# A tokens' norm summed in four column groups, and the order of the first weight loads

## The chip, the cores and the metric

The kernel runs on one core of a Trainium2 chip. The metric is device time in microseconds of one execution, and lower is better. A core has five engines that run side by side: PE (the matrix engine TensorE, whose weight loads the profile lists apart as PEld), DVE (VectorE), ACT (ScalarE), POOL (GpSimd) and SP (SyncE, which here only issues transfers). Transfers between device memory and on-chip memory run on 16 DMA engines that all queues share. Matmuls write to PSUM, from where DVE and ACT read.

## What is computed

One layer of a block for a generator over latent tokens: 512 tokens of width 2048, and 256 context tokens. Only the head of it matters here:

```python
shift, scale, gate = jnp.split(silu_c @ w_ada[l] + b_ada[l], 3, axis=-1)
shift_c, scale_c, gate_c = jnp.split(silu_cc @ w_ada[l] + b_ada[l], 3, axis=-1)
h = _modulate(_rmsnorm(xs, norm_g[l]), shift[:, None], scale[:, None])
hc = _modulate(_rmsnorm(cs, norm_g[l]), shift_c, scale_c)
...
p = h @ w_l
```

`_rmsnorm` divides each token by the root of the mean of its squares over the 2048 columns, and `_modulate` is `h * (1 + scale) + shift`. Everything behind it (attention with normalised and rotated heads, a Fourier mixer, gates, two projections, a residual add and a last norm) reads `p`, and is not touched by the change.

## The kernel before

Tokens are held transposed: `xt` has the 2048 columns in 16 blocks (`kb`) of 128 partitions, with the 512 tokens along the free axis. All matmuls of the projections run as three passes (`mm3`, lines 251 to 253): each operand is split in a high and a low part (`split_from`, lines 131 and 132: ACT copies the high part, DVE subtracts), and high x high, high x low and low x high are added in PSUM.

The first stage, up to about 215 us, makes `h` block by block and at once multiplies it with the first 14 tiles of the input projection. For each `kb` it needs the following.

- The tokens' norm, once for all blocks. `squares` (line 385) squares the 16 blocks of `xt`, 13 on ACT (line 394) and three on DVE (392), adds them in pairs on DVE (395) and sums over the partitions with eight matmuls against a matrix of ones (397), which leaves each token's sum on all 128 partitions. ACT takes the square root (404) and DVE the reciprocal (405), over 128 x 512 numbers.
- The shift and the gain of the block's 128 columns. `modulation(kb)` multiplies a modulation matrix of 2 MB, loaded in two halves (`wada_load`, line 365, four buffers), with the two conditioning vectors: `matvec` (line 425) uses 32 columns of the array for each of four matmuls. ACT copies the result (432), two transposes turn it to columns (435), DVE sums and scales (439, 487, 488).
- `make_h` (line 412): DVE multiplies the tokens by gain and norm (`ht`, 414), ACT adds the shift for the high part (415), DVE makes the low part (416).

`start_work` then runs the projection's tiles for the groups of blocks of which `h` is complete (1, 1, 2, 4, 4 and 4 blocks), with weights that come as `start` pieces through `start_load` (line 162, on SP's queue, four raw buffers) and are split by lines 131 and 132. Its results are kept by lines 453 and 455.

`warm` (line 445) issues matmuls whose product is never read. In block 0 there are three behind the matrix products and five behind the transposes.

The order of instructions on each engine is set when the program is built, by a scheduler; each engine then works through its own list in order and waits where an operand isn't there. PE's list before is: eight norm matmuls, the first matrix in two halves, three unread products, two transposes, five unread products, the first half of the second matrix, then the first projection tiles. SP's list is: the small vectors, `xt` in six pieces, the first matrix, three start pieces, the second matrix, and then a further start piece whenever a raw buffer is free. The matrices from the third on come through POOL's queue, two blocks ahead, each when PE has freed a buffer.

Of the kernel before, what the change touches and what calls it, by code (L numbers as in the profile page):

```python
# [10 lines left out]
F32 = mybir.dt.float32  # L11
F32R = mybir.dt.float32r
ACT = mybir.ActivationFunctionType
ALU = mybir.AluOpType
# [4 lines left out]
P = 128  # L19
D = 2048  # L20
T = 512
C = 256
KK = D // P
# [38 lines left out]
    f = {"P1": "Z5", "P2": "S2", "Q6": "S3", "P7": "S4"}.get(name)  # L62
    return [(f, pc - 1)] if f and g == 0 and pc in (1, 2) else []

XCH = [(0, 2), (2, 2), (4, 4), (8, 4), (12, 2), (14, 2)]


def start_pieces():
# [15 lines left out]
def block_kernel(ctx, tc, xT, ctxT, x, c_row, w_ss, w_gate, vecs, qkg, rope, dft_c, dft_s,  # L84
                 w_start, w_kv, w_m, w_g, w_pab, w_o, final_g, out):
    nc = tc.nc
    sb = lambda name, bufs=1, side="left": ctx.enter_context(tc.tile_pool(name=name, bufs=bufs, side=side))

    def region(name, side="left", **kw):
        st = ExitStack()  # L90
        return st, st.enter_context(tc.tile_pool(name=name, bufs=1, side=side, **kw))
# [18 lines left out]
    def uid(s):  # L110
        cnt[0] += 1
        return f"{s}{cnt[0]}"
# [3 lines left out]
    def slot(pool, shape, dt=F32):  # L116

        n = turns[pool] = turns.get(pool, -1) + 1
        return pool.tile([P] + list(shape), dt, tag=f"s{n % KK}", bufs=1, name=uid("s"))

    def hm_tile(shape, dt, name):
        return slot(hm, shape[1:], dt)

    def bank(shape=(P, 512)):
        return ps.tile(list(shape), F32, tag="b1", bufs=4, name=uid("pb"))

    def bank2():
        return ps.tile([P, 1024], F32, tag="b2", bufs=2, name=uid("pd"))
# [6 lines left out]
    todo, ahead = [], []  # L135
# [16 lines left out]
    def start_load():  # L152

        e = todo[0]
        used = [p for a in ahead for p, _ in a.raws]
        free = [p for p in raw_pools for _ in range(p[1] - used.count(p))]
        if len(e.parts) > len(free) or e.stage == 0 and (not chain or left[e.pc]):
            return False
        todo.pop(0)
        for p, src in zip(free, e.parts):  # L160
            raw = p[0].tile([P, 1024], F32, tag=p[2], bufs=p[3], name=uid("wr"))[:, : e.cols]
            nc.sync.dma_start(raw, src)
            e.raws.append((p, raw))
        if e.stage == 0:
            nc.sync.dma_start(chain[e.pc], e.first)
            left[e.pc] = 1
        ahead.append(e)
        return True
# [89 lines left out]
    ones = const.tile([P, P], F32, name="ones")  # L258
# [3 lines left out]
    eps_t = const.tile([P, 1], F32, name="eps_t")  # L262
# [4 lines left out]
    cvt, bada, ng = small[:, : 2 * KK], small[:, 2 * KK : 5 * KK], small[:, 5 * KK :]  # L267
# [8 lines left out]
    hhi = [None] * KK  # L276
    hlo = [None] * KK
# [51 lines left out]
    for g in range(4):  # L329
        for name in ONE_GROUP:  # L330
            stream_product(name, g, w_g[g], BY_DVE_GATES)
            if g >= 2 and name in DONE:
                half, c = DONE[name]
# [8 lines left out]
    for name in OUT_GROUP:  # L342
        stream_product(name, 4, w_o[1], BY_DVE_OUT)
        if name in DONE:
            half, c = DONE[name]
            stream(("x", half, 2 + c), flat(x[half, 2 + c]), 1024, 1, "raw")
    for name in ONE_GROUP:
        stream_product(name, 5, w_o[0], BY_DVE_OUT)
        half, c = {"P2": (0, 0), "P7": (1, 1), "Q3": (1, 0)}.get(name, (0, 0))
# [12 lines left out]
    pa, pap = region("pa", "right")  # L362
    xt = pap.tile([P, KK, T], F32, name="xt")

    def wada_load(kb, h):
        w = pap.tile([P, 8, 256], F32, tag="wada", bufs=4, name=uid("wa"))
        (nc.gpsimd if kb > 1 else nc.sync).dma_start(w, w_ss[kb, :, 8 * h : 8 * h + 8, :])
        return w

    for a, n in XCH:  # L370
        nc.sync.dma_start(xt[:, a : a + n, :], xT[:, a : a + n, :])


    c2 = pap.tile([P, KK, 32], F32, name="c2")
    nc.vector.memset(c2, 0.0)
    rt = pap.tile([P, 1], F32, name="rt")
    ce = pap.tile([P, 2 * KK], F32, name="ce")
    nc.scalar.activation(ce, cvt, ACT.Exp, scale=-1.0)
    nc.scalar.activation(rt, ce[:, 0:1], ACT.Sqrt)
    nc.vector.tensor_scalar(ce, ce, 1.0, None, op0=ALU.add)  # L380
    nc.vector.reciprocal(ce, ce)
    nc.vector.tensor_tensor(c2[:, :, 0:2].rearrange("p k j -> p j k"),
                            cvt.rearrange("p (j k) -> p j k", j=2),
                            ce.rearrange("p (j k) -> p j k", j=2), op=ALU.mult)
    def squares(srcs, n, r, new, run=None):

        acc = bank2()
        for q in range(0, KK, 2):
            a, b = new(), new()
            for t, src in zip((a, b), srcs(q)):  # L390
                if run is None and t is b and q in (4, 8, 10):
                    nc.vector.tensor_tensor(t, src, src, op=ALU.mult)
                else:
                    nc.scalar.activation(t, src, ACT.Square)
            nc.vector.tensor_tensor(a, a, b, op=ALU.add)
            if run is None:
                nc.tensor.matmul(acc[:, :n], ones, a, start=q == 0, stop=q == KK - 2)
            elif q == 0:
                nc.vector.tensor_copy(run, a)
            else:  # L400
                nc.vector.tensor_tensor(run, run, a, op=ALU.add)
        if run is not None:
            nc.tensor.matmul(acc[:, :n], ones, run, start=True, stop=True)
        nc.scalar.activation(r, acc[:, :n], ACT.Sqrt, bias=eps_t[:, 0:1], scale=1.0 / D)
        nc.vector.reciprocal(r, r)

    wada = {(0, h): wada_load(0, h) for h in range(2)}
    while todo and len(ahead) < 3:
        start_load()
    wada.update({(1, h): wada_load(1, h) for h in range(2)})  # L410

    def make_h(hi, lo, src, rr, kb, j, pool, n):
        tmp = pool.tile([P, n], F32, tag="htmp", bufs=2, name=uid("ht"))
        nc.vector.scalar_tensor_tensor(tmp, src, gain[:, kb, j : j + 1], rr, op0=ALU.mult, op1=ALU.mult)
        nc.scalar.activation(hi, tmp, ACT.Identity, bias=shift[:, kb, j : j + 1])  # L415
        nc.vector.scalar_tensor_tensor(lo, tmp, shift[:, kb, j : j + 1], hi.bitcast(F32),  # L416
                                       op0=ALU.add, op1=ALU.subtract)

    def matvec(acc, pieces):

        kk = 0
        for w in pieces:
            for k in range(w.shape[1]):
                j = kk % 4
                nc.tensor.matmul(acc[32 * j : 32 * j + 32, :256], c2[:, kk, :], w[:, k, :],
                                 start=kk < 4, stop=kk >= KK - 4)
                kk += 1

    def columns(acc, kb):

        o = pap.tile([P, 256], F32, tag="ada_o", bufs=2, name=uid("ado"))
        nc.scalar.copy(o, acc[:, :256])
        sp = acc[:, 512:768]
        for i in range(2):
            nc.tensor.transpose(sp[:, P * i : P * i + P], o[:, P * i : P * i + P], ident)
        if kb == 0:
            warm(5, o)
        r = pap.tile([P, 2, 2], F32, tag="ada_r", bufs=2, name=uid("adr"))
        nc.vector.tensor_reduce(r, sp.rearrange("p (h g r) -> p h r g", h=2, g=4)[:, :, 0:2, :], axis=AX.X, op=ALU.add)
        return r  # L440

    def warm(n, src):

        for _ in range(n):
            nc.tensor.matmul(wacc[:, :256], ones, src, start=True, stop=True)

    def start_work():
        ends = {kb + nk for kb, nk in GROUPS}
# [32 lines left out]
    def modulation(kb):  # L481
        acc = bank2()
        matvec(acc, pieces := [wada.pop((kb, h), None) or wada_load(kb, h) for h in range(2)])
        if kb == 0:
            warm(3, pieces[1][:, 7, :])
        sp = columns(acc, kb)
        nc.vector.tensor_scalar(shift[:, kb, :], sp[:, 0, :], bada[:, kb : kb + 1], None, op0=ALU.add)
        nc.vector.tensor_scalar(gain[:, kb, :], sp[:, 1, :], bsc1[:, kb : kb + 1], ng[:, kb : kb + 1],
                                op0=ALU.add, op1=ALU.mult)

    wacc = bank()
    rx = pap.tile([P, T], F32, name="rx")
    squares(lambda q: (xt[:, q, :], xt[:, q + 1, :]), T, rx, lambda: hm_tile([P, 2, T], F32, name=uid("sq"))[:, 0, :])
    modulation(0)

    work = start_work()
    done = 0
    for kb in range(KK):
        if kb:
            modulation(kb)  # L500
        if kb % 2 == 0:
            pairs.append([hm_tile([P, 2, T], F32R, name=uid(n)) for n in ("hh", "hl")])
        hhi[kb], hlo[kb] = (t[:, kb % 2, :] for t in pairs[-1])
        make_h(hhi[kb], hlo[kb], xt[:, kb, :], rx, kb, 0, pap, T)

        full = max([k + n for k, n in GROUPS if k + n <= kb] or [0])
        owed = 42 * full
        lim = min(owed, done + 48)
        while done < lim:
            done += next(work)  # L510
# [88 lines left out]
    for g in range(4):  # L599
        gate_b(g)  # L600
        positions(g)
        if g < 2:
            channels(g + 2)
    squares(ct_load, C, rc, lambda: crp.tile([P, C], F32, tag="sq", bufs=4, name=uid("sq")),
            crp.tile([P, C], F32, name="run"))
    crs.close()
# [66 lines left out]
    for which, half in ((0, 0), (0, 1), (1, 1)):  # L673
        toks = range(3 * half, 3 * half + 3) if which == 0 else (4, 5)
        b = bank2()
        accs = [b[:, :512], b[:, 512:], bank()]
        for pc in range(8):
# [9 lines left out]
            if keys and pc in (1, 3, 5):  # L687
                a, t = keys.pop(0)
# [3 lines left out]
        for a, t in zip(accs, toks):  # L692
            a = a.rearrange("p (h d) -> p h d", h=4)
# [222 lines left out]
    acc = bank()  # L916
# [70 lines left out]
    for i in range(NSTEP + 2):  # L987
# [9 lines left out]
        if i % 3 > 0 and i < 3 * KK:  # L997
            q = i // 3 * 2 + i % 3 - 1
# [3 lines left out]
        if i % 3 < 2 and i < 3 * KK:  # L1002
            q = i // 3 * 2 + i % 3
# [354 lines left out]
```

## Time and profile before

| | us |
|---|---|
| median of 3 runs | 1386.96 (1386.47 to 1394.96) |
| the profiled execution's own time | 1388.98 |
| its span, first to last instruction | 1387.2 |

The page gives the busy time of each engine, where the sum over engines says nothing: they overlap. Rows of the timeline read "start, length, engine, line, operation, output<-inputs, tile, how many merged", and in brackets how long the engine was idle before and what ended that. A matmul's length is longer than its share of the array, since matmuls follow each other before the last one has drained; the distance of two starts is what one costs. One fp32 matmul of the source is two passes, so two rows, while the three passes of `mm3` are one row each. Rows of the windows read "from:to length, PE busy, PEld busy, DVE, ACT, POOL, granted clock of PE, share of the DMA engines' time, GB/s", each busy time with its number of instructions.

Transfers by issuing line, with the median time from issue to landing:

```profile
wa<-in_w_ss POOLq DMA_DIRECT2D x28, 1024.0 KB, 8.3
wr<-in_w_start SPq DMA_DIRECT2D x26, 512.0 KB, 6.4
wa<-in_w_ss SPq DMA_DIRECT2D x4, 1024.0 KB, 13.3
xt<-in_xT SPq DMA_DIRECT2D x4, 512.0 KB, 7.2
xt<-in_xT SPq DMA_DIRECT2D x2, 1024.0 KB, 7.8
```

`wa` are the halves of the modulation matrices, `wr` the raw weights. The first four `wa` go through SP, the other 28 through POOL.

### The profile page before, as it was taken

How to read it: one execution, taken by the hardware profiler on the slowest of the kernel's cores; microseconds unless marked ns; L12 is line 12 of the kernel's file. 1: busy time of each engine (PE TensorE's matmuls, PEld its weight loads, DVE VectorE, ACT ScalarE, POOL GpSimd, SP SyncE). 2: the span in 40 equal slices, each digit the busy share in tenths (PEclk: the TensorE clock that was granted, in tenths of full speed). 3: DMA queues.
4: the chain of work that ended last, by engine and by line, in shares of the span. 5: the costliest groups of instructions: out<-in, count | busy, mean ns of one | idle time of the engine just before them, and what ended most of it. 6: DMA issues, size and time to landing. Idle time of an engine off the chain costs nothing. (4 is left out here: it accounts for less than half of the span.)

```text
span 1387.2 us, 17607 instructions
## 1 busy us (share of the span) xinstructions
PE 1351.4 (97%) x6810; PEld 1107.1 (80%) x6810; DVE 910.7 (66%) x1191; ACT 630.1 (45%) x861; POOL 116.8 (8%) x173
## 2 busy tenths in 40 slices
PE   7999999999999999999999999999999999999986
PEld 4667789888888888888887788888888788878865
DVE  5765486767865668656743776665956546487577
ACT  5322253534545454554544555444544224364434
POOL 0110000011100001000001101000010100020100
PEclk9999999999999999999999999999999999999998
DMA  9887453645443335433447998989898844588973
GB/s 384 330 343 263 168 186 108 185 122 186 153 145 113 116 113 161 140 98 121 124 143 271 326 291 239 258 226 258 263 269 296 310 152 136 136 184 274 238 220 131
DMA packets 76115, 283.67 MB, mean 204 GB/s; under 512 B 8704, under 2 KB 9344, under 8 KB 71680
## 3 DMA queue, kind: packets, MB, share of 16 engines
q1 hardware_dynamic: 52848, 185.28, 39.9%
q0 software_dynamic: 18000, 79.71, 21.2%
q10 hardware_dynamic: 5184, 17.57, 3.3%
q8 instruction: 53, 0.87, 0.3%
q14 instruction: 30, 0.25, 0.1%
HBM read 257.34 MB, written 25.17 MB: 204 GB/s over the span
## 5 line engine op out<-in xcount | busy, mean ns | idle before, releaser
L131 ACT ACTIVATE whi<-wr 128x1024 fp32r<-128x1024 f32 x178 | 185.0, 1043 | 292.7 <-PE pb L252 84.0
L132 DVE TENSOR_TENSOR wlo<-wr,whi 128x1024 fp32r<-128x1024 f32 x178 | 213.4, 1202 | 140.7 <-ACT whi L131 140.5
L251 PE MATMUL pb<-s,whi 128*128 128x512 f32 x512 | 206.7, 405 | 0.6 <-ACT s L415 0.6
L252 PE MATMUL pb<-s,whi 128*128 128x512 f32 x512 | 200.6, 392 | 0.1
L253 PE MATMUL pb<-s,wlo 128*128 128x512 f32 x512 | 200.5, 392 | 0.0
L252 PE MATMUL y<-wlo,s 128*128 128x512 f32 x320 | 127.2, 397 | 7.3 <-DVE wlo L132 7.2
L251 PE MATMUL x<-whi,s 128*128 128x512 f32 x324 | 127.3, 393 | 2.2 <-ACT whi L131 1.1
L252 PE MATMUL x<-wlo,s 128*128 128x512 f32 x324 | 127.2, 393 | 1.9 <-DVE wlo L132 1.9
L251 PE MATMUL y<-whi,s 128*128 128x512 f32 x320 | 126.8, 396 | 0.8 <-ACT whi L131 0.6
L253 PE MATMUL x<-whi,s 128*128 128x512 f32 x324 | 126.9, 392 | 0.0
L253 PE MATMUL y<-whi,s 128*128 128x512 f32 x320 | 126.4, 395 | 0.0
L251 PEld LDWEIGHTS pb<-s,whi 128*128 128x128 f32 x512 | 96.1, 188 | 21.7 <-issue 4.1
L253 PEld LDWEIGHTS pb<-s,wlo 128*128 128x128 f32 x512 | 96.1, 188 | 21.1 <-issue 0.4
L252 PEld LDWEIGHTS pb<-s,whi 128*128 128x128 f32 x512 | 96.4, 188 | 17.1 <-DVE s L416 1.0
L131 ACT ACTIVATE whi<-R 128x1024 fp32r<-128x1024 f32 x66 | 69.6, 1058 | 66.6 <-PE x L253 38.4
L132 DVE TENSOR_TENSOR wlo<-R,whi 128x1024 fp32r<-128x1024 f32 x66 | 80.0, 1219 | 20.5 <-ACT whi L131 20.4
L955 ACT ACTIVATE p<-pd,mx 128x768 f32<-128x768 f32 x48 | 43.2, 899 | 84.9 <-DVE mx L953 84.9
L252 PEld LDWEIGHTS y<-wlo,s 128*128 128x128 f32 x320 | 61.2, 191 | 22.9 <-DVE wlo L132 10.2
L251 PEld LDWEIGHTS x<-whi,s 128*128 128x128 f32 x324 | 61.3, 189 | 16.2 <-ACT whi L131 1.5
L252 PEld LDWEIGHTS x<-wlo,s 128*128 128x128 f32 x324 | 61.2, 189 | 15.2 <-DVE wlo L132 2.6
L251 PEld LDWEIGHTS y<-whi,s 128*128 128x128 f32 x320 | 61.1, 191 | 14.5 <-ACT whi L131 1.0
L253 PEld LDWEIGHTS x<-whi,s 128*128 128x128 f32 x324 | 61.3, 189 | 12.8
(270 smaller groups left out, 2663.7 us busy)
## 6 DMA issues: line engine op xcount, KB each, us to landing
wr<-in_w_g SPq DMA_DIRECT2D x80, 512.0 KB, 8.2
wa<-in_w_ss POOLq DMA_DIRECT2D x28, 1024.0 KB, 8.3
wr<-in_w_m SPq DMA_DIRECT2D x44, 512.0 KB, 3.8
wr<-in_w_gate SPq DMA_DIRECT2D x32, 512.0 KB, 3.6
wr<-in_w_pab SPq DMA_DIRECT2D x32, 512.0 KB, 4.3
R<-in_w_g POOLq DMA_DIRECT2D x32, 512.0 KB, 10.1
wr<-in_w_o SPq DMA_DIRECT2D x32, 512.0 KB, 5.2
wr<-in_w_start SPq DMA_DIRECT2D x26, 512.0 KB, 6.4
```

What stands on the lines that cost most here:

```text
L131: nc.scalar.activation(hi, src, ACT.Copy)
L132: nc.vector.tensor_tensor(lo, src, hi.bitcast(F32), op=ALU.subtract)
L251: nc.tensor.matmul(o, ah, bh, start=start, stop=False, skip_group_check=cont)
L252: nc.tensor.matmul(o, ah, bl, start=False, stop=False, skip_group_check=cont)
L253: nc.tensor.matmul(o, al, bh, start=False, stop=stop, skip_group_check=cont)
L955: nc.scalar.activation(p, sc[:, :NKEY], ACT.Exp, bias=mx[:, 0:1], accum_out=mx[:, 1:2])
```

## The change

Three things are changed in the first stage.

- The norm. `token_norms` takes the place of `squares` (which stays for the context). Each of the 16 blocks is squared (11 on ACT, five on DVE) and goes to PE without being added to another. There it takes four matmuls, one for each quarter of 128 tokens, each with 32 columns of ones, so that the sums of the four quarters land on four groups of 32 partitions, 128 columns wide. Square root and reciprocal then run over 128 x 128 numbers. Four full-width matmuls with a selecting matrix (`pick`, set by POOL) spread them to 128 partitions x 512 tokens in PSUM. Block 0's `make_h` reads that PSUM bank; ACT copies it to `rx` for the other blocks.
- The unread products. One of 128 columns stands behind each of the first 14 blocks of squares, and four of 256 columns behind the last. Behind the first matrix one is left of three. The five behind the transposes stay.
- The loads. `xt`'s last piece is cut in two. The first three modulation matrices go through SP's queue, the first start piece between the first and second matrix, three more between the second and third. POOL loads from the fourth matrix on.

```diff
-XCH = [(0, 2), (2, 2), (4, 4), (8, 4), (12, 2), (14, 2)]
+XCH = [(0, 2), (2, 2), (4, 4), (8, 4), (12, 2), (14, 1), (15, 1)]
...
-        (nc.gpsimd if kb > 1 else nc.sync).dma_start(w, w_ss[kb, :, 8 * h : 8 * h + 8, :])
+        (nc.gpsimd if kb > 2 else nc.sync).dma_start(w, w_ss[kb, :, 8 * h : 8 * h + 8, :])
...
+    wada = {(0, h): wada_load(0, h) for h in range(2)}
+    start_load()
+    wada.update({(1, h): wada_load(1, h) for h in range(2)})
+    for _ in range(3):
+        start_load()
+    wada.update({(2, h): wada_load(2, h) for h in range(2)})
...
-    wada = {(0, h): wada_load(0, h) for h in range(2)}
-    while todo and len(ahead) < 3:
-        start_load()
-    wada.update({(1, h): wada_load(1, h) for h in range(2)})
+    def token_norms():
+
+        t = hm_tile([P, 2, T], F32, name=uid("nm"))
+        pick, r = t[:, 0, :].rearrange("p (t c) -> p t c", t=4), t[:, 1, :P]
+        nc.gpsimd.memset(pick, 0.0)
+        for t in range(4):
+            nc.gpsimd.memset(pick[32 * t : 32 * t + 1, t, :], 1.0)
+        acc = bank()
+        for kb in range(KK):
+            if kb % 2 == 0:
+                two = hm_tile([P, 2, T], F32, name=uid("sq"))
+            sq = two[:, kb % 2, :]
+            if kb % 3 == 2 or kb == KK - 2:
+                nc.vector.tensor_tensor(sq, xt[:, kb, :], xt[:, kb, :], op=ALU.mult)
+            else:
+                nc.scalar.activation(sq, xt[:, kb, :], ACT.Square)
+
+            for t in range(4):
+                nc.tensor.matmul(acc[32 * t : 32 * t + 32, :P], ones[:, :32], sq[:, t * P : t * P + P],
+                                 start=kb == 0, stop=kb == KK - 1)
+            if kb < KK - 2:
+                warm(1, sq[:, :P])
+        warm(4, sq[:, :256])
+        nc.scalar.activation(r, acc[:, :P], ACT.Sqrt, bias=eps_t[:, 0:1], scale=1.0 / D)
+        nc.vector.reciprocal(r, r)
+        acc = bank()
+        for t in range(4):
+            nc.tensor.matmul(acc[:, t * P : t * P + P], pick[:, t, :], r, start=True, stop=True)
+        return acc
...
-            nc.tensor.matmul(wacc[:, :256], ones, src, start=True, stop=True)
+            nc.tensor.matmul(wacc[:, : src.shape[-1]], ones, src, start=True, stop=True)
...
-            warm(3, pieces[1][:, 7, :])
+            warm(1, pieces[1][:, 7, :])
...
-    squares(lambda q: (xt[:, q, :], xt[:, q + 1, :]), T, rx, lambda: hm_tile([P, 2, T], F32, name=uid("sq"))[:, 0, :])
+    rx0 = token_norms()
     modulation(0)
...
-        make_h(hhi[kb], hlo[kb], xt[:, kb, :], rx, kb, 0, pap, T)
+        make_h(hhi[kb], hlo[kb], xt[:, kb, :], rx if kb else rx0, kb, 0, pap, T)
+        if kb == 0:
+            nc.scalar.copy(rx, rx0)
```

In the instruction lists of the changed program PE has, one after the other: for each block of squares its four 32-wide matmuls and, up to the 14th, an unread product; four unread products; the four that spread the reciprocal; both halves of the first matrix; one unread product; two transposes; five unread products; four matmuls of four projection tiles on the high parts; the first half of the second matrix; and then the low parts of those tiles. DVE's split of the first start piece stands behind block 0's `ht`. The squares and what follows take nine of the 16 rotating buffers of `h` instead of 16, so `h` starts at the tenth. Behind the first 200 instructions or so of each engine the lists are the same but for three places much later, where one instruction stands two or three positions further on.

More of the change, by code (lines that the diff above doesn't have):

```diff
@@ L376, in block_kernel @@
     rt = pap.tile([P, 1], F32, name="rt")
+    ex = pap.tile([P, 2 * KK], F32, name="ex")
     ce = pap.tile([P, 2 * KK], F32, name="ce")
-    nc.scalar.activation(ce, cvt, ACT.Exp, scale=-1.0)
-    nc.scalar.activation(rt, ce[:, 0:1], ACT.Sqrt)
-    nc.vector.tensor_scalar(ce, ce, 1.0, None, op0=ALU.add)
+    nc.scalar.activation(ex, cvt, ACT.Exp, scale=-1.0)
+    nc.scalar.activation(rt, ex[:, 0:1], ACT.Sqrt)
+    nc.vector.tensor_scalar(ce, ex, 1.0, None, op0=ALU.add)
     nc.vector.reciprocal(ce, ce)
@@ L384, in block_kernel, with squares @@
                             ce.rearrange("p (j k) -> p j k", j=2), op=ALU.mult)
-    def squares(srcs, n, r, new, run=None):
+    def squares(srcs, n, r, new, run):
         acc = bank2()
@@ L390, in squares @@
             for t, src in zip((a, b), srcs(q)):
[L391 to L394, printed above, removed]
+                nc.scalar.activation(t, src, ACT.Square)
             nc.vector.tensor_tensor(a, a, b, op=ALU.add)
-            if run is None:
-                nc.tensor.matmul(acc[:, :n], ones, a, start=q == 0, stop=q == KK - 2)
-            elif q == 0:
+            if q == 0:
                 nc.vector.tensor_copy(run, a)
@@ L401, in squares @@
                 nc.vector.tensor_tensor(run, run, a, op=ALU.add)
-        if run is not None:
-            nc.tensor.matmul(acc[:, :n], ones, run, start=True, stop=True)
+        nc.tensor.matmul(acc[:, :n], ones, run, start=True, stop=True)
         nc.scalar.activation(r, acc[:, :n], ACT.Sqrt, bias=eps_t[:, 0:1], scale=1.0 / D)
         nc.vector.reciprocal(r, r)
-    wada = {(0, h): wada_load(0, h) for h in range(2)}
-    while todo and len(ahead) < 3:
-        start_load()
-    wada.update({(1, h): wada_load(1, h) for h in range(2)})
+    def token_norms():
[25 more added lines that the diff above has]
+        return acc
     def make_h(hi, lo, src, rr, kb, j, pool, n):
```

## The prediction

> **What bounds the kernel now.** I read the page's busy table first, then the windows, to see where TensorE (PE) is not busy.
>
> ```profile
> PE 1351.4 (97%) x6810; PEld 1107.1 (80%) x6810; DVE 910.7 (66%) x1191; ACT 630.1 (45%) x861; POOL 116.8 (8%) x173
> ...
> 0.00:25.61 25.61, 16.01 (x82) 8.07 (x83) 14.92 (x29) 13.86 (x23) 2.19 (x9) 1.00 0.93 373
> 25.61:37.64 12.03, 11.56 (x60) 8.24 (x61) 4.48 (x8) 8.54 (x17) 0.80 (x2) 1.00 1.01 412
> 37.64:100.00 62.36, 61.31 (x448) 41.65 (x448) 44.40 (x77) 18.54 (x28) 8.25 (x16) 1.00 0.86 333
> 100.00:1387.00 1287.00, 1262.57 (x6223) 1049.18 (x6221) 846.93 (x1078) 589.11 (x795) 105.61 (x148) 0.99 0.63 193
> ```
>
> PE is busy 97% of the span, and 98% from 37.64 us on. Only ahead of 25.61, where the first projection matmul (L251) starts, does it lack work: 9.6 us idle. (37.64 is where it takes up the third modulation matrix.) A change to the first stage is therefore worth what it moves the moment T0 = 25.61, plus the gaps up to 37.64; from there PE carries the shift to the end. The timeline shows what T0 waits for:
>
> ```profile
> 17.55 1.07 PE L425 MATMUL pd<-wa,c 128*32 128x256 f32 x16
> 17.66 0.69 ACT L404 ACTIVATE rx<-pd,eps_t 128x512 f32<-128x512 f32 x1 [2.60 <-PE pd L397]
> 18.38 3.35 DVE L405 RECIPROCAL rx<-rx 128x512 f32<-128x512 f32 x1 [2.59 <-ACT rx L404]
> 18.87 1.07 PE L425 MATMUL pd<-wa,c 128*32 128x256 f32 x16 [0.25 <-DMA wa<-in_w_ss]
> 21.27 0.38 PE L435 MATMUL pd<-ident,ado 128*128 128x128 f32 x2
> 21.48 2.32 PE L445 MATMUL pb<-ado,ones 128*128 128x256 f32 x10
> 24.06 0.74 DVE L414 SCALAR_TENSOR_TENSOR ht<-xt,gain,rx 128x512 f32<-128x512 f32 x1
> 24.84 0.72 ACT L415 ACTIVATE s<-ht,shift 128x512 fp32r<-128x512 f32 x1 [2.68 <-DVE ht L414]
> 25.61 0.73 PE L251 MATMUL pb<-s,whi 128*128 128x512 f32 x2 [0.59 <-ACT s L415]
> ```
>
> Two chains meet in `ht` at 24.06. The norm goes through the reciprocal, which holds VectorE until 21.73. The modulation goes through the second half of the first matrix, which lands at 18.87 and is multiplied by 19.94. The reciprocal is late, and the weight splits queued behind it push `ht` to 24.06.
>
> **What the change saves.** The reciprocal shrinks from 512 columns to 128. A 32-column one bounds it from below:
>
> ```profile
> 7.58 0.35 DVE L381 RECIPROCAL ce<-ce 128x32 f32<-128x32 f32 x1
> ```
>
> On the straight line between 0.35 and 3.35 us, 128 columns take 0.95. The square root (0.69 for 512) takes 0.35 by my estimate, at most 0.69. VectorE loses its eight additions of squares and gets five squares. Its split of the first weight now stands behind `ht`, so nothing is queued in front of the modulation. What the modulation then needs after its products, block 1 shows without a reciprocal in its way:
>
> ```profile
> 28.93 1.07 PE L425 MATMUL pd<-wa,c 128*32 128x256 f32 x16 [0.42 <-DMA wa<-in_w_ss]
> 30.06 0.37 ACT L432 COPY ado<-pd 128x256 f32<-128x256 f32 x1 [1.16 <-PE pd L425]
> 30.73 0.38 PE L435 MATMUL pd<-ident,ado 128*128 128x128 f32 x2
> ...
> 31.88 0.75 DVE L414 SCALAR_TENSOR_TENSOR ht<-xt,gain,rx 128x512 f32<-128x512 f32 x1
> 32.79 0.72 ACT L415 ACTIVATE s<-ht,shift 128x512 fp32r<-128x512 f32 x1
> ```
>
> From the end of the products (30.00): copy done 30.43, transpose 0.02 later if PE is free, then 1.15 over the reduction to `ht`, 0.91 to ACT, and 0.77 to PE (24.84 to 25.61): 3.3 us. With the products done at 19.94 as now, T0 would be 23.25, a gain of 2.4. PE is free: of the three unread products behind the first matrix one is left (0.43, and 0.2 for the change of width below), and it ends with the copy. `ht` now reads the norm from PSUM; the nearest row is another such operation with one operand there,
>
> ```profile
> L581 DVE SCALAR_TENSOR_TENSOR bb<-pb,part x4: 628/692/693, 224.2 to 234.9; 128x512 f32<-128x512 f32 x4
> ```
>
> 0.69 against 0.74, so I cost it at nothing.
>
> **What the change adds on PE.** In PE's new order each of 16 tiles of squares brings four matmuls on 32 columns of the array each (two passes, so eight instructions), and 14 tiles are followed by an unread full-width product of 128 columns. Four 256-column products come behind the last tile, then four full-width matmuls that spread the reciprocal, and only then, in PE's order, both halves of the first matrix. Each piece is priced from a row.
>
> A round of four 32-wide matmuls of 256 columns takes 0.23 us: sixteen passes in 1.07, each lasting 0.38, so (1.07 - 0.38) / 3. Ten full-width passes of 256 columns in 2.32 give (2.32 - 0.38) / 9 = 0.216 each. At 128 columns I take 0.108 for both (two transposes of 128 columns in 0.38, each 0.27 long, are 0.11 apart). So a tile streams for 4 x 0.108 = 0.43. But going from full width to 32-wide and back costs extra. Here one 32-wide matmul (two passes) stands between full-width ones:
>
> ```profile
> 45.11 0.39 PE L253 MATMUL pb<-s,wlo 128*128 128x512 f32 x1
> 45.43 0.62 PE L425 MATMUL pd<-wa,c 128*32 128x256 f32 x2
> 45.98 0.50 PE L251 MATMUL pb<-s,whi 128*128 128x512 f32 x1
> 46.31 0.39 PE L252 MATMUL pb<-s,whi 128*128 128x512 f32 x1
> 46.54 0.39 PE L253 MATMUL pb<-s,wlo 128*128 128x512 f32 x1
> ```
>
> Undisturbed full-width matmuls start 0.23 apart (46.31 to 46.54). From 45.11 to 46.31 are 1.20 us for two of them (0.46) and two 256-column passes (0.43): 0.31 to 0.32 are the two changes of width. A tile then costs 0.43 + 0.32 = 0.75 us of PE. The Trainium skill ("TensorEngine Tiling (Array Packing)", Tiling Modes) says that changing the mode, unlike changing the tile, drains TensorE; it gives no price, and the 0.32 here agrees with it. Its table of theoretical speedup ("up to 4x" for 32 columns, same page, Overview) leaves the drain out; by that alone the sum would be that of the second case below.
>
> How fast do the squares come?
>
> ```profile
> 5.18 0.63 ACT L394 ACTIVATE s<-xt 128x512 f32<-128x512 f32 x1 [2.46 <-DMA xt<-in_xT]
> 7.23 3.38 ACT L394 ACTIVATE s<-xt 128x512 f32<-128x512 f32 x6
> ...
> 13.91 1.15 ACT L394 ACTIVATE s<-xt 128x512 f32<-128x512 f32 x2
> ```
>
> Tile 0 is ready at 5.8, tile 1, which ACT takes up at 7.23, at 7.9. ACT then makes one every 0.56 (3.38 / 6) and VectorE five of the 16, with the last at about 14.7. So squares come faster than 0.75 apart, and from 7.9 on PE is behind: 13 tiles x 0.75 + 0.46 for the last two (without a product) end at 18.1 at best. And PE starts at half speed:
>
> ```profile
> 11.35 0.34 PEld L397 LDWEIGHTS pd<-s,ones 128*128 128x128 f32 x1 [0.52 <-DVE s L395]
> 12.20 0.29 PEld L397 LDWEIGHTS pd<-s,ones 128*128 128x128 f32 x1 [0.52 <-issue]
> 12.74 0.19 PEld L397 LDWEIGHTS pd<-s,ones 128*128 128x128 f32 x1 [0.24 <-issue]
> 13.17 0.19 PEld L397 LDWEIGHTS pd<-s,ones 128*128 128x128 f32 x1 [0.24 <-issue]
> ```
>
> Passes are 0.85 apart before about 12.4 and 0.43 after, though the windows print a granted clock of 1.00 there: the rise came less than 4 us after PE began. At low clock a tile costs 1.18 (only streaming doubled) to 1.5 (all doubled); I take 1.35, the middle. The rise I put at 10.4, the middle of 8.7 to 12.1, since tile 0 starts at 5.85 and a pause follows. By then 2.5 / 1.35 = 1.9 tiles are done instead of 3.3: 1.1 us lost, the sums end at 19.2.
>
> **The sum.** 19.2; four unread products 8 x 0.216 + 0.2 for the change = 1.9, to 21.1, which hide square root and reciprocal (19.5 + 0.35 + 0.95 = 20.8; without that cover the path would still wait for 20.8); the spread 8 x 0.108 = 0.87, to 22.0; both halves of the matrix, landed by 18.9, 8 x 0.216 + 0.12, the last pass 0.16 longer: 24.0; 3.3 to T0 = 27.3, **1.7 later** than now. Behind T0 the first half of the second matrix, now multiplied before it, comes after: +0.86 + 0.32 = +1.18. Two of today's gaps go. One is the wait between the pair at 25.61 and the next matmul:
>
> ```profile
> 26.40 0.50 PE L252 MATMUL pb<-s,whi 128*128 128x512 f32 x1
> ...
> 28.12 0.39 PE L251 MATMUL pb<-s,whi 128*128 128x512 f32 x1
> ```
>
> 26.40 - 25.61 - 2 x 0.23 = 0.3: PE now has four matmuls on the high half to do while the low half is made. The other is the late half at 28.93: 28.93 - 28.12 - 0.32 = 0.49. It was loaded in competition with GpSimd's queue; on one queue it ends 9.0 MB of transfers, and at the 373 GB/s of the first 25.61 us that is 24.0 by my estimate. Together +0.4. The rest is free. With the DMA share at 0.93 to 25.61, one more issue on SP delays no landing. SP's loads of the third matrix wait until PE frees the first one's buffers, and SP's next weights queue behind them; both are used from 37.64 on. The copy of the norm on ACT stands ahead of copies whose matmuls end later. GpSimd, busy 2.19 of 25.61 us, has its memsets done early. What is late next if T0 does come early: nothing, PE has blocks to do. **Sum: +2.1 us**, on the profiled execution's 1388.98 (span 1387.2 plus 1.8 around it) 1391.1. That execution is 2.0 above the median 1386.96, so I forecast 1389.1.
>
> **The rivals.** *Widths change for less* (the other side): if the next 32-wide loads slip under the unread product, PE keeps pace with the squares, the landing at 18.87 sets T0 = 23.25, and -2.4 + 0.4 = -2.0 gives 1385.0. It decides below 0.13 us a pair: break-even is T0 = 25.2, 2.1 earlier over some 11 tiles at 0.32. For it: no row repeats such changes every 0.75 us, so this rhythm is not shown. Against it: 0.32 came out with the next matmul ready.
>
> *The clock stays low.* Three windows of 3.4 us, with PE's busy time and the clock:
>
> ```profile
> 794.00:797.40 3.40, 2.01 (x9) 1.31 (x7) 1.55 (x2) 1.37 (x2) 0.00 (x0) 1.00 0.41 166
> 1080.80:1084.20 3.40, 1.89 (x7) 1.04 (x6) 3.40 (x3) 1.86 (x2) 0.00 (x0) 1.00 0.50 135
> 1084.20:1087.60 3.40, 3.40 (x9) 2.63 (x9) 1.82 (x3) 2.00 (x2) 0.00 (x0) 0.50 0.73 239
> 1343.60:1347.00 3.40, 2.04 (x5) 1.66 (x6) 3.40 (x4) 1.06 (x1) 0.00 (x0) 0.50 0.53 170
> 1347.00:1350.40 3.40, 3.40 (x10) 2.63 (x9) 3.40 (x4) 2.35 (x3) 0.00 (x0) 0.50 0.83 288
> ```
>
> A window 56% busy was followed by half clock, one 59% busy was not, and 60% at half clock did not raise it. A tile at low clock streams 0.86 of 1.35 us, 64%: close. Then 13 x 1.35 + 0.9 from 7.9 end at 26.3, and T0 falls 6 to 11 us late: about +9, 1396. The Trainium skill ("TensorE: Matmul & The Clock Gate", Part 1) has the clock set by windows of 3.4 us that run free of the kernel; the rows agree in length, and by it the rise moves from run to run.
>
> *It does nothing*: the DMA share is 1.01 to 37.64, so the landings might set the pace whatever T0 is: 1387. Against it: PE is 96% busy there, and only 0.5 us waits for a transfer.
>
> **Chances and range.** Forecast 0.58, own range 1387.9 to 1390.8 (T0 26.5 to 28.6). Cheaper change 0.22, at 1384.2 to 1386. Low clock 0.12, at 1394 to 1400. Nothing 0.08. The range 1384.3 to 1391.5 leaves out the low clock and some edge. 1% (13.9 us) is what can be told from no change; only the low clock at its worst comes near: faster 0.01, same 0.96, slower 0.03.
>
> **What would show it.** In the timeline: full-width after 32-wide at 0.75 us a tile, PE without idle time from 8 to 24, the spread at about 21, the first L251 near 27.3. If PE waits for ACT between tiles, or the matrix at 18.87 starts on its landing, the second case holds; passes of 0.21 up to 20 us mean the third.

## The result and the profile after

The changed kernel takes 1402.74 us (median of 4 runs, 1401.6 to 1404.74), against 1387.62 for the kernel before (median of 4, the ones shown earlier and one more). The ratio is 1.0102, with a 95% interval of 1.008 to 1.0125: slower by 14 us by the ratio and 15 by the medians, 1%, where 1389.1 was forecast. The profiled execution took 1402.41, with a span of 1400.6.

The busy table of the page, changed kernel:

```profile
PE 1364.7 (97%) x6962; PEld 1115.9 (80%) x6962; DVE 906.5 (65%) x1185; ACT 628.8 (45%) x860; POOL 117.0 (8%) x176
```

PE's busy time rose by 13.3 us (from 1351.4), nearly the whole 13.4 by which this execution is longer. PE is thus not waiting more, it is busy longer. The timeline of the changed kernel shows with what, and on what T0 now hangs:

```profile
8.20 0.65 PE L426 MATMUL pb<-s,ones 128*32 128x128 f32 x8 [0.65 <-ACT s L423]
8.78 0.80 PE L471 MATMUL pb<-s,ones 128*128 128x128 f32 x2
9.51 0.66 PE L426 MATMUL pb<-s,ones 128*32 128x128 f32 x8
...
14.34 0.63 ACT L423 ACTIVATE s<-xt 128x512 f32<-128x512 f32 x1 [0.16 <-DMA xt<-in_xT]
...
23.95 0.66 PE L426 MATMUL pb<-s,ones 128*32 128x128 f32 x8
24.54 0.80 PE L471 MATMUL pb<-s,ones 128*128 128x128 f32 x2
25.27 1.08 PE L426 MATMUL pb<-s,ones 128*32 128x128 f32 x16
26.28 2.94 PE L471 MATMUL pb<-s,ones 128*128 128x256 f32 x8
26.41 0.37 ACT L431 ACTIVATE s<-pb,eps_t 128x128 f32<-128x128 f32 x1 [11.45 <-PE pb L426]
26.81 0.95 DVE L432 RECIPROCAL s<-s 128x128 f32<-128x128 f32 x1 [12.43 <-ACT s L431]
29.05 1.05 PE L435 MATMUL pb<-s 128*128 128x128 f32 x8
30.03 1.93 PE L451 MATMUL pd<-wa,c 128*32 128x256 f32 x32
32.03 0.37 ACT L458 COPY ado<-pd 128x256 f32<-128x256 f32 x1 [5.25 <-PE pd L451]
33.68 0.75 DVE L440 SCALAR_TENSOR_TENSOR ht<-xt,gain,pb 128x512 f32<-128x512 f32 x1
34.46 0.72 ACT L441 ACTIVATE s<-ht,shift 128x512 fp32r<-128x512 f32 x1 [1.10 <-DVE ht L440]
35.24 1.21 PE L251 MATMUL pb<-s,whi 128*128 128x512 f32 x4 [0.18 <-ACT s L441]
```

T0 is 35.24, 9.63 later than the 25.61 before. The squares are not the reason: ACT's last one ends at 14.97. From 8.20 on a tile (L426 and its unread product, L471) comes every 1.31 us, still at 23.95, and ACT waits 11.45 us for the sums, which are done at 26.3. The lengths tell the clock: the fourteenth unread product is as long (0.80) as the second. Half clock ends inside the row at 26.28: its eight passes and one change of width take 2.77 to the next start at 29.05, against 8 x 0.216 + 0.2 = 1.9 at full clock; about four of the eight were slow, which puts the rise near 28.2. The trace's own record of the clock has it at 28.2 too, and at 12.4 for the kernel before.

The windows of the changed kernel (PE, PEld, DVE, ACT, POOL busy, granted clock, DMA share, GB/s) don't show this:

```profile
15.00:20.00 5.00, 5.00 (x40) 2.62 (x32) 0.00 (x0) 0.00 (x0) 0.00 (x0) 1.00 1.03 421
20.00:25.00 5.00, 5.00 (x41) 2.78 (x40) 0.00 (x0) 0.00 (x0) 0.00 (x0) 1.00 0.99 403
```

PE reads as 5.00 of 5.00 busy, at a granted clock printed as 1.00 though passes take twice their time. ACT and DVE do nothing from 15 to 25 us. A row's length also holds the draining of its last pass (in e3 below, the first row is 0.66 long and the next starts 0.42 later), so "busy" here means that some matmul is under way, not that columns stream.

Behind T0 the shift grows from 9.63 to 11.4 by about 90 us, where PE waits for a half matrix at the same place as before (the same matmul, first in the timeline before, then in the changed kernel's):

```profile
89.14 1.07 PE L425 MATMUL pd<-wa,c 128*32 128x256 f32 x16 [0.94 <-DMA wa<-in_w_ss]
...
100.54 1.07 PE L451 MATMUL pd<-wa,c 128*32 128x256 f32 x16 [1.07 <-DMA wa<-in_w_ss]
```

From there the same matmul stays 11.4 to 11.7 later up to 700 us. Between 700 and 745 us (by the trace before) this grows to 14.4: PE waits 1.33 and 0.61 us for parts of a split there, and the clock is low from 741.6 to 745.0 by the trace's record. Then comes a wait that the trace before doesn't have, again with a low clock around it (775.7 to 782.6; 0.80 for a matmul that takes 0.39 at full clock). It is given back: the same matmul is 18.0 later behind it and 14.5 later from 790 us on. From 1088 to 1220 us it is 13.4 later: ahead of that, at 1084.2, the execution before has a stretch of half clock (the prediction shows it) that no other trace here has.

```profile
777.64 0.80 PE L251 MATMUL x<-whi,s 128*128 128x512 f32 x1 [5.56 <-ACT ev L926]
```

### The profile page after: what moved, and what is told of

Same layout as the page of the kernel before. It is cut to its first block, busy times and chain, and to the rows that moved or that the text cites. A ratio compares the mean times of both kernels' runs of the same rounds, so it can differ in the third digit from the quotient of the medians.

```text
span 1400.6 us, 17911 instructions
## 1 busy us (share of the span) xinstructions
PE 1364.7 (97%) x6962; PEld 1115.9 (80%) x6962; DVE 906.5 (65%) x1185; ACT 628.8 (45%) x860; POOL 117.0 (8%) x176
## 5 line engine op out<-in xcount | busy, mean ns | idle before, releaser
L251 PE MATMUL pb<-s,whi 128*128 128x512 f32 x512 | 206.5, 405 | 0.2 <-ACT s L441 0.2
L251 PE MATMUL x<-whi,s 128*128 128x512 f32 x324 | 127.7, 394 | 6.7 <-ACT ev L926 5.6
L251 PE MATMUL y<-whi,s 128*128 128x512 f32 x320 | 125.8, 393 | 0.4 <-ACT s L852 0.2
L251 PEld LDWEIGHTS pb<-s,whi 128*128 128x128 f32 x512 | 96.1, 188 | 21.9 <-issue 3.3
L132 DVE TENSOR_TENSOR wlo<-R,whi 128x1024 fp32r<-128x1024 f32 x66 | 80.1, 1220 | 19.7 <-ACT whi L131 19.7
L251 PEld LDWEIGHTS x<-whi,s 128*128 128x128 f32 x324 | 61.4, 189 | 20.4 <-ACT ev L926 6.0
L251 PEld LDWEIGHTS y<-whi,s 128*128 128x128 f32 x320 | 60.5, 189 | 13.7 <-ACT whi L131 0.6
```

The source lines that it names most:

```text
L132: nc.vector.tensor_tensor(lo, src, hi.bitcast(F32), op=ALU.subtract)
L251: nc.tensor.matmul(o, ah, bh, start=start, stop=False, skip_group_check=cont)
```

## The experiments

My theory: in this rhythm PE streams only two thirds of the time, that doesn't raise the clock, and the half clock is the loss. The rivals: the loads and the buffers (later landings, `h` from another buffer), and the changes of width by themselves. The kernels of each group ran on one chip, beside runs of the kernel before there (median 1386.42 in the first group, 1386.61 in the second). The time and place of each come first, since every experiment is read from them. The fourth column is the start of the half matrix that the kernel before multiplies at 89.14; the clock's rise is from the trace's record.

| kernel | clock rises | first L251 | that half matrix | median | ratio to before (95%) |
|---|---|---|---|---|---|
| before | 12.4 | 25.61 | 89.14 | | |
| changed | 28.2 | 35.24 | 100.54 | 1402.74 | 1.0102 (1.008 to 1.0125) |
| e1, loads alone | 12.7 | 25.08 | 87.68 | 1387.13 | 0.9998 (0.9986 to 1.0009) |
| e2, no products between tiles | 11.9 | 24.59 | 88.67 | 1385.89 | 0.9996 (0.9986 to 1.0006) |
| e3, products of the tiles' width | 12.7 | 24.92 | 89.00 | 1386.02 | 0.9995 (0.9986 to 1.0004) |
| e4, a burst ahead | 4.7 | 26.39 | 90.84 | 1388.9 | 1.0021 (1.0008 to 1.0034) |
| f1, e3 with a delay | 10.7 | 38.05 | 99.01 | 1395.97 | 1.0075 (1.0061 to 1.0089) |
| f2, longer products | 13.3 | 31.84 | 97.09 | 1397.16 | 1.0081 (1.0067 to 1.0094) |
| f3, changed, again | 29.4 | 35.58 | 101.00 | 1399.11 | 1.0098 (1.0085 to 1.0112) |
| f4, before from the tenth buffer | 11.8 | 25.80 | 88.96 | 1385.88 | 0.9996 (0.9985 to 1.0006) |

### e1: the loads alone

The kernel before, with the change's loads and nothing else:

```diff
-XCH = [(0, 2), (2, 2), (4, 4), (8, 4), (12, 2), (14, 2)]
+XCH = [(0, 2), (2, 2), (4, 4), (8, 4), (12, 2), (14, 1), (15, 1)]
-        (nc.gpsimd if kb > 1 else nc.sync).dma_start(w, w_ss[kb, :, 8 * h : 8 * h + 8, :])
+        (nc.gpsimd if kb > 2 else nc.sync).dma_start(w, w_ss[kb, :, 8 * h : 8 * h + 8, :])
...
+    wada = {(0, h): wada_load(0, h) for h in range(2)}
+    start_load()
+    wada.update({(1, h): wada_load(1, h) for h in range(2)})
+    for _ in range(3):
+        start_load()
+    wada.update({(2, h): wada_load(2, h) for h in range(2)})
```

> The kernel before with the change's loads alone (last piece of xt in two, first three matrices on SP's queue with the start pieces between them); norm and unread products as before. My theory (all of the loss is in the norm's work on PE at half clock): the first projection matmul stays at 25.6 us, the wait of 0.5 us for the second matrix goes, time ratio to before 0.9997 (0.999 to 1.001). Rival (the loads cost what the changed kernel lost behind its first block, 3 to 5 us between 42 us and the end): ratio 1.002 to 1.0035.

T0 came 0.53 earlier and the time is the same. The loads, and the queue they go through, are not where the 15 us went.

### e2 and e3: without the changes of width

e2 leaves out the 14 unread products between the tiles. e3 keeps them, but in the width of the tiles, as four matmuls on 32 columns each:

```diff
             if kb < KK - 2:
-                warm(1, sq[:, :P])
+                for t in range(4):
+                    nc.tensor.matmul(wacc[32 * t : 32 * t + 32, :P], ones[:, :32], sq[:, t * P : t * P + P],
+                                     start=True, stop=True)
```

> The changed kernel without the 14 unread products between the tiles of squares, so no change of width until the last tile. My theory (the changes of width keep the array too little streamed to raise the clock, and make a tile cost 1.31 us): a tile takes about 0.45 us even at half clock, the sums are done at about 15.7 instead of 26.3, the four unread products then run at half clock to about 19.5, the clock rises between 18.9 and 22.3, the first projection matmul starts at 26.3 to 27.8 instead of 35.2; ratio 1.001 to 1.004, the upper part if the later stages keep their 2 to 4 us. Rival (the 32-wide matmuls themselves cost 1.31 us a tile at half clock): the first projection matmul stays behind 33 us, ratio above 1.007.

> The changed kernel with each of the 14 unread products between the tiles replaced by four 32-wide ones of the same columns: the same streaming time, no change of width. My theory: at half clock a tile takes 0.86 us without a pause, the clock rises by about 12.5 us, then PE keeps pace with the squares, sums done at 15 to 16, first projection matmul at 23.3 to 24.5; ratio 0.998 to 1.000, or up to 1.002 if the later stages lose 2 to 4 us all the same. Rival (the clock wants full-width work, or longer products): half clock through the norm, sums at 19.5, first projection matmul at about 30, ratio 1.003 to 1.006.

Timeline of e2:

```profile
7.92 1.51 PE L426 MATMUL pb<-s,ones 128*32 128x128 f32 x24 [1.38 <-ACT s L423]
9.63 1.94 PE L426 MATMUL pb<-s,ones 128*32 128x128 f32 x32 [0.20 <-ACT s L423]
...
20.25 1.07 PE L449 MATMUL pd<-wa,c 128*32 128x256 f32 x16 [1.29 <-DMA wa<-in_w_ss]
...
24.59 1.19 PE L251 MATMUL pb<-s,whi 128*128 128x512 f32 x4 [0.17 <-ACT s L439]
```

Timeline of e3, where L430 are the unread products:

```profile
5.75 0.66 PE L426 MATMUL pb<-s,ones 128*32 128x128 f32 x8 [5.75 <-ACT s L423]
6.17 0.65 PE L430 MATMUL pb<-s,ones 128*32 128x128 f32 x8
7.78 0.66 PE L426 MATMUL pb<-s,ones 128*32 128x128 f32 x8 [0.95 <-ACT s L423]
...
8.63 0.65 PE L426 MATMUL pb<-s,ones 128*32 128x128 f32 x8
...
9.49 0.65 PE L426 MATMUL pb<-s,ones 128*32 128x128 f32 x8
...
13.25 0.39 PE L426 MATMUL pb<-s,ones 128*32 128x128 f32 x8
13.46 0.39 PE L430 MATMUL pb<-s,ones 128*32 128x128 f32 x8
13.68 0.39 PE L426 MATMUL pb<-s,ones 128*32 128x128 f32 x8
...
24.92 1.19 PE L251 MATMUL pb<-s,whi 128*128 128x512 f32 x4 [0.17 <-ACT s L443]
```

e3 does the same amount of streaming as the changed kernel and its clock rises at 12.7; T0 is 24.92 and the loss is gone. Its rows also give what a tile streams: 0.86 at half clock (8.63 to 9.49) and 0.43 at full (13.25 to 13.68). The changed kernel's 1.31 at half clock is then 0.86 of streaming and 0.45 for two changes of width, a share of 66%. T0 is later than the 23.3 to 24.5 that I had expected of e3: its sums end at 17.0 and not at 15 to 16.

e2 went better than I expected. I had looked for a late rise behind the norm; but tiles of 0.43 follow each other there (rows from 7.92 to 9.43 and from 9.63 to 11.57, the last 0.2 of each being the draining), which in the 3.4 us before 11.9 makes 2.5 us of streaming, 73%, and that was enough. T0 is then set by the landing at 20.25, not by the norm. With the clock up, the two kernels that keep the new norm are as fast as the one before, no more: T0 is 0.7 to 1.0 earlier (0.5 with the loads alone, in e1), and the half matrix 0.1 to 0.5.

### e4: full clock ahead of the norm

The changed kernel, with eight full-width unread products of 256 columns ahead of the first tile, on a buffer that GpSimd fills:

```diff
+    nc.gpsimd.memset(part[:, 0, :256], 1.0)
+    warm(8, part[:, 0, :256])
     rx0 = token_norms()
```

> The changed kernel with eight full-width unread products of 256 columns ahead of the norm, on a tile that GpSimd fills with ones, from about 2 to 8 us when PE has no work; all else as changed. My theory: the clock is up when the squares come, a tile with its two changes of width costs 0.75 us, sums at 18 to 19, first projection matmul at 26 to 27.5, ratio 1.000 to 1.003. It leaves open whether the clock holds through the norm, where the array streams 0.43 of 0.75 us; if it falls back, the first projection matmul starts at 29 to 33. Rival (a change of width has a fixed price whatever the clock, and the half clock is not the cause): first projection matmul at 33 or later, ratio above 1.007.

Timeline of e4:

```profile
1.24 5.41 PE L471 MATMUL pb<-part,ones 128*128 128x256 f32 x16 [1.24 <-POOL part L519]
...
12.38 0.43 PE L426 MATMUL pb<-s,ones 128*32 128x128 f32 x8
12.74 0.49 PE L471 MATMUL pb<-s,ones 128*128 128x128 f32 x2
13.15 0.43 PE L426 MATMUL pb<-s,ones 128*32 128x128 f32 x8
...
17.80 0.65 PE L426 MATMUL pb<-s,ones 128*32 128x128 f32 x16
18.38 1.99 PE L471 MATMUL pb<-s,ones 128*128 128x256 f32 x8
20.20 1.05 PE L435 MATMUL pb<-s 128*128 128x128 f32 x8
21.19 1.93 PE L451 MATMUL pd<-wa,c 128*32 128x256 f32 x32
23.05 0.70 PE L471 MATMUL pb<-wa,ones 128*128 128x256 f32 x2
...
26.39 1.20 PE L251 MATMUL pb<-s,whi 128*128 128x512 f32 x4 [0.17 <-ACT s L441]
```

Nothing of the change is taken away here, and T0 comes 8.9 us earlier than in the changed kernel's profile and 9.2 earlier than in f3's: of 9.6 and 10.0 us of lateness, 0.8 is left. The half clock is the loss, shown by giving it back alone. T0 is still 1.5 to 1.8 us later than in e3 and e2, and the changes of width are what e4 has more: a tile takes 0.775 (12.38 to 13.15), of which 0.43 streams. That is 56%, for nine microseconds, and the clock held.

### f1, f2, f3 and f4: what a delay is worth, and how much streaming is enough

f1 is e3 with a longer row of unread products behind the last tile: a late T0 at full clock. f2 is the changed kernel with longer products between the tiles. f3 is the changed kernel once more, and f4 the kernel before with `h` started at the tenth of its rotating buffers, as the change does. The three edits in this order, f1's against e3, f2's against the changed kernel, f4's against the one before:

```diff
-        warm(4, sq[:, :256])
+        warm(28, sq[:, :256])
...
-                warm(1, sq[:, :P])
+                warm(1, sq[:, :256])
...
+    turns[hm] += 9
     modulation(0)
```

> The kernel with unread products of the same width, and 28 instead of four full-width unread products of 256 columns behind the last tile of squares: PE is held up by 24 x 2 x 0.216 = 10.4 us at full clock, so that the first projection matmul starts at about 35.3 us as in the changed kernel, without the low clock and with the same lists of instructions behind it. My theory (the later stages lose what the first stage loses, no more): 0.9995 + 10.4 / 1386.4 gives a ratio of 1.007 (1.006 to 1.008). Rival (a first stage that is 10 us late costs another 4 to 5 us later, which would explain all of the changed kernel's 1.0102): ratio 1.010 to 1.011.

> The changed kernel with the 14 unread products between the tiles at 256 columns instead of 128. The array then streams 1.28 of 1.73 us a tile at half clock (74%), where the changed kernel streamed 0.86 of 1.31 (66%). If a share between 66% and 74% is what raises the clock: it rises by about 12 us, a tile then costs 0.97, sums at 22 to 23, first projection matmul at about 31, ratio 1.004 to 1.007. If it takes more than 74%: half clock through the norm, sums at 31, first projection matmul at 39 to 41, ratio 1.012 to 1.016. My theory doesn't say which; a rival in which the shorter products alone cost the time expects the first.

> The changed kernel once more, beside the others on one chip. My theory: half clock to about 28 us again, first projection matmul at 34.5 to 37, ratio 1.010 to 1.012. Rival (the low clock was a chance of where the clock's windows fell): first projection matmul at 27 to 29 in this profile, ratio below 1.006.

> The kernel before with h starting at the tenth of the 16 rotating buffers, as in the changed kernel; nothing else. The changed kernel and all its variants so far show one wait of 4 to 6 us for ACT near 757 us that the kernel before lacks. If the buffers bring that wait, it is here too; by the variants with a clock that rose it is given back by about 800 us, so my theory expects a ratio of 1.000 (0.999 to 1.001). Rival (it is not given back and makes up for what the changed kernel lost beyond its first stage): ratio 1.002 to 1.004.

In f1's timeline 56 unread passes stand between 17.44 and 29.63, 48 more than in e3, and the first L251 comes at 38.05, before which PE had done both halves of the second matrix (0.55 us from 33.11 and 1.86 from 36.19), which the others do behind it; so its list there is not the changed kernel's, against what I had expected. At the half matrix it is 9.87 late, still 9.9 at 700 us and 10.1 at 1200, and its median is 9.4 above the one before. A delay of the first stage is paid once, to the end. f4 shows no cost for the other start of the buffers.

Timeline of f2:

```profile
9.97 0.66 PE L426 MATMUL pb<-s,ones 128*32 128x128 f32 x8
10.55 1.22 PE L471 MATMUL pb<-s,ones 128*128 128x256 f32 x2
11.70 0.66 PE L426 MATMUL pb<-s,ones 128*32 128x128 f32 x8
...
13.41 0.43 PE L426 MATMUL pb<-s,ones 128*32 128x128 f32 x8
13.76 0.70 PE L471 MATMUL pb<-s,ones 128*128 128x256 f32 x2
14.39 0.43 PE L426 MATMUL pb<-s,ones 128*32 128x128 f32 x8
```

Here the changes of width are the same 28, but a tile streams 0.43 + 0.86 = 1.29 of 1.73 (9.97 to 11.70), 74%, and the clock rises at 13.3. So it is not the change of width as such that holds the clock down, but the share that is left. e3 says the same from the other side: from 5.9 to 9.3 it has no change of width, but a pause, so that about 2.25 of 3.4 us stream, 66%, and the clock did not rise at the end of that window. The longer products cost their own time (0.98 a tile at full clock, 13.41 to 14.39, against 0.775): T0 is 31.84, and the time, at 1.0081, is worse than I had written for this case.

f3 repeats the result: tiles of 1.31 us up to 24.8, and the clock rises only in the row of unread products behind them, at 29.4.

```profile
24.82 1.08 PE L426 MATMUL pb<-s,ones 128*32 128x128 f32 x16
25.83 3.73 PE L471 MATMUL pb<-s,ones 128*128 128x256 f32 x8
29.39 1.05 PE L435 MATMUL pb<-s 128*128 128x128 f32 x8
```

## Why the prediction was wrong

**The step that failed** is "The rise I put at 10.4, the middle of 8.7 to 12.1, since tile 0 starts at 5.85 and a pause follows." It took the rise to come within about four microseconds of steady work, as in the kernel before, whose matmuls start at 8.63 (the row below) and whose clock rises at 12.4, and gave no row for 8.7 and 12.1. But before, 512-column passes stream without a break (0.85 apart at half clock, twice the 0.43 of full); in the new rhythm a tile streams 66%, and the clock did not rise before 28.2 (29.4 in f3), when the unread full-width products came. The half clock was priced at 1.1 us; between the changed kernel and e4 it is 8.9 at T0. The prediction had the number that speaks against this step, 64% streaming at half clock beside a window of 60% that did not raise the clock, and gave it a chance of 0.12 as a rival. Its windows count busy time, though, not streaming, and of the three two began at full clock and only the 60% one at half, the state in which the kernel starts. Keeping the clock and gaining it are two questions: e4 keeps it with 56% of streaming, the changed kernel doesn't gain it with 66%.

```profile
8.63 8.99 PE L397 MATMUL pd<-s,ones 128*128 128x512 f32 x16 [8.63 <-DVE s L395]
```

**What the forecast would have been without that step.** It held 1.1 us of lateness for the half clock, so T0 = 27.3 - 1.1 = 26.2 with the clock up. e4, which has the clock up, measured 26.39. Up to T0 the other terms were thus right, within 0.2 us in sum. In time that sum gives +1.0 (0.6 at T0 and 0.4 behind it), while e4 is 1.7 later at the half matrix and 2.5 in its median (1.1 to 4.7 by its interval): the 0.4 was too small. Term by term up to T0, in the rows of e4 above:

- a tile 0.75: 0.775; the sums end at 18.1: 18.4;
- four unread products 1.9: 1.82 (18.38 to 20.20); the spread 0.87: 0.99, with the change of width; the matrix 1.85: 1.86 (21.19 to 23.05, where the next row starts);
- from the matrix to T0 3.3: 3.34.

In the changed kernel itself, the reciprocal of 128 columns was put at 0.95 and took 0.95, the square root at 0.35 and took 0.37, `ht` with the norm in PSUM at nothing more, and took 0.75. A tile at half clock was put at 1.35 and took 1.31. The landing of the first matrix cost no wait in the profiled execution.

**The rivals.** The rival with the low clock is what came: sums at 26.3, as it said, and T0 9.63 late, inside its 6 to 11. Its 1394 to 1400 was still too low for the first four runs, and holds f3's median. *Widths change for less* needed a price below 0.13 a pair; it is 0.34 (0.775 - 0.43) at full clock and 0.45 at half. The Trainium skill ("TensorEngine Tiling (Array Packing)", Tiling Modes) says that a change of mode drains TensorE, and these are the prices of two such drains here. *It does nothing* fell too, since T0 decides and a delay goes through to the end.

**The sum behind T0** was +0.4, and it was mis-sized too. It counted one more pair of changes of width. In the new lists the halves of the matrices mostly stand apart between projection matmuls: from T0 to the same matmul, at 67.98 in the kernel before and 79.31 in the changed one, PE does them in 12 groups (also in e2, e3, e4, f2 and f3) where the kernel before has seven, so five pairs of changes more. Four pairs at the prediction's 0.32 are 1.3 us on top of the 0.4, which makes 1.7; the traces have 1.6 to 2.0 over that stretch. f1 bears the price out: with six groups and two half matrices less than e3 in that stretch, it takes 3.7 us less, of which the halves are 1.7 and each group is 0.33. That at the half matrix e2 and e3 have lost only 0.55 and e4 0.9 is luck with an early T0: the kernel before waits 0.94 there for the landing, e2 and e3 don't wait and e4 only 0.2. The late ones wait 1.1 to 1.3 and keep the whole loss: 1.8 (changed), 1.9 (f3) and 1.7 (f2).

**What stays open.** The medians of the changed kernel are 15.1 above the one before in the first four runs and 12.5 in f3, of which 11.4 and 11.9 stand at the half matrix; f2 has 10.6 of which 7.9, f1 9.4 of which 9.9. So what arises later goes from nothing to almost 4 us, with intervals of about 2 to 3 us to each side, and was not settled. Single executions of one kernel differ as much: in f3's the same matmul is 12.5 later at 1020 us and 9.1 at 1200, where the changed kernel's has 14.5 and 13.4. The wait that ends at 777.64 in the changed kernel, 5.6 long, is in every kernel with the new norm (4.2 in e2, 3.9 in e3, 5.4 in e4), but only 0.3 long in e1 with the loads alone and absent in f4 with the buffers alone. It is given back by 790 us (in f1 all but 0.6 of it); why the norm brings it stays open.

## What to carry to other kernels

Unread matmuls meant to raise TensorE's clock have to raise the share of time in which columns stream, and a short product of another width than its neighbours can leave it too low: in e3 products of the same 128 columns in the neighbours' width have the clock up 15 us earlier. Before a rhythm of small matmuls is put at the start of a kernel, divide the streaming of one round by its period, at half clock, and compare that with a stretch of the trace that raised the clock, not with the busy time. A shorter norm ahead of the first projection was worth 0.7 to 1.0 us at T0 (e2, e3), of which the loads alone bring 0.5 (e1), and nothing that the time shows. And an order that splits work of one width into more groups pays for each: five more pairs of changes are about 1.6 us behind T0 here.

## What the hardware showed that I had not expected

In these runs the clock's rise goes by the share of streaming. Counted back from each rise in steps of 3.4 us, with 0.43 us of streaming for a tile at half clock and as much for its product (0.86 in f2), windows at half clock with 60% to 67% did not raise it (changed; also f2 from 6.5 to 9.9 and e3 from 5.9 to 9.3), nor did f3's last one before the rise, about 69%; 73% (e2), 74% to 76% (f2) and more did. At full clock 56% was enough to keep it (e4). The prediction's window that was 56% busy and lost the clock is no counterexample: its matmuls, five of 0.22 us and part of a sixth, stream about 1.3 of 3.4 us, 38%. The Trainium skill ("TensorE: Matmul & The Clock Gate", Part 1) gives a budget of about 3.4 us of sustained activity, whatever the number of matmuls, and full clock behind it; in the changed kernel PE shows no idle time from 8.20 on and stayed at half clock for 20 us, so that rule holds here only where "activity" is read as streaming. And the granted clock that the windows print is no witness before the first rise: it says 1.00 at 15 to 25 us, where only the length of the passes tells the half clock.
